# Gate products in three passes, modulations in batches of four, norms spread by transposes: a change to a two-layer diffusion backbone on one Trainium2 core

## The chip, the core and the metric

The kernel runs on one core of a Trainium2 chip. Its engines work in parallel, each through its own queue in order: TensorE (PE; its weight loads are listed apart as PEld), VectorE (DVE), ScalarE (ACT), GpSimd (POOL), and SyncE (SP), whose queue issues nearly all DMA transfers here. PE multiplies a stationary operand that is loaded first by a moving one and writes to banks of PSUM. The metric is device time in microseconds of one execution, the median of several runs; lower is better.

## The reference

The model has two layers over 512 latent tokens and 256 context tokens of width 1024. Each layer computes

```python
mod_x = (silu_c @ ada_w[l] + ada_b[l])[:, None, :]
sh1, sc1, gt1, sh2, sc2, gt2 = jnp.split(mod_x, 6, axis=-1)
mod_c = silu_cc @ ada_w[l] + ada_b[l]
...
ux = modulate(rmsnorm(x, norm1_g[l]), sh1, sc1) @ w_in[l]
uc = modulate(rmsnorm(ctx, norm1_g[l]), csh1, csc1) @ w_in[l]
...
mix_x = jnp.concatenate(
    [conformer_conv(ux[..., :CONV_IN], *cv), rwkv_out(yx, prep_x, *post)],
    axis=-1).astype(x.dtype)
...
x = x + gt1 * (mix_x @ w_out[l])
x = x + gt2 * swiglu(modulate(rmsnorm(x, norm2_g[l]), sh2, sc2),
                     ffn_wg[l], ffn_wu[l], ffn_wd[l])
```

`conformer_conv` is a depthwise convolution of 31 taps with a group norm; `rwkv_out` normalizes the output of a two-directional recurrence over the tokens by heads, adds a bonus, and multiplies by a gate `g = sigmoid(g_lo) @ g_up`, a product over 160 values (the head gate). The context has the same path in layer 0, and only feeds the recurrence's state in layer 1. A last RMS norm ends it. All values are float32.

Three pieces matter below: the modulations (`silu(c) @ ada_w`, for c and c_ctx at once: a product with two rows and 6144 columns in each layer), the head gate, and the norms, whose factor per token has to reach all 128 partitions.

## The kernel before

Activations lie with channels on partitions and tokens along the free dimension: 8 tiles of 128 channels by 768 tokens. Large products are made of three passes over rounded parts: an operand is split into a high part (`act` to a rounded type) and a low part (`tt`, the difference), and high x high, high x low and low x high are added up in PSUM (`dense`, `win`, `project`). Products given as plain float32 appear as two PE records for each call. `mm` (L234), `act` (L222), `stt` (L225), `tt` (L228) and `ts` (L231) are helpers, so those lines stand for nearly all instructions; tile names tell them apart.

The order of time, with the stages of the profile in us from its start:

- 0 to 75: inputs, norm, first modulations, first three input projections of layer 0.
- 75 to 645: layer 0's recurrent stage. Twelve batches (four pairs of heads by three token groups); a function `weave` interleaves lanes of PE work at positions written out in `PLAN`: the recurrence's steps (`chains`, 12 a batch), inversion of small triangular blocks, token transposes, input projections, convolutions, norms, modulations (`ada`, a number of steps for each batch). Inside `tc.manual_schedule` PE runs in exactly this order; the other engines' orders, and everything outside, come from a list scheduler that takes program order as priority. Toward the end `mix_early` multiplies by the head gates and `out_early` begins the output projection.
- 645 to 732: rest of the output projection, second norm, modulation, first feed-forward tile (outside the manual order).
- 732 to 1262: layer 0's feed-forward, in parts of 6, 6, 5 and 5 of its 22 tiles. For each tile f there are two products (gate and up, 24 x 2 PE products each), whose weight tiles (512 KB) are loaded by SP into two buffers and split by ACT and DVE into two more.
- 1262 to 2250: the same for layer 1 (recurrent stage 1310 to 1832, feed-forward from about 1876 on).

The parts that the change touches:

- Modulations (`ada_load` L280, `ada_sums`, `ada_cols`, `ada_steps`). The 48 column groups of 128 in each layer are computed one by one. SP loads a group's weights (128 partitions x 1024, 512 KB) in one DMA. `ada_sums` makes eight products with 32 stationary columns (c and c_ctx in two of them) over 128 moving columns; product k goes to partitions 32(k mod 4) onward of one bank, so that the eight partial sums stand in four places. ACT copies the bank to `ev`. `ada_cols` multiplies `ev` by `sel` (a 0/1 matrix with two columns), which adds the four places and turns columns into partitions, and DVE adds the bias (and for scales forms (1 + scale) x norm gain). A step of the generator is one of these two halves. Part 0 (16 groups: shift and scale before the mixer), part 1 (8, mixer's gate), part 2 (16, before the feed-forward), part 3 (8, feed-forward's gate). Layer 0's part 0 runs in the first stage; its parts 1 and 2 and layer 1's part 0 (40 groups) as a lane of layer 0's recurrent stage; layer 1's parts 1 and 2 (24) in its own; part 3 of each layer (`gates`, six buffers) is placed ahead of the feed-forward and run by `run(gates)`.
- Norms (`spread`, called by `rstd`, `gn`, `pair_prep`). A norm's sums are taken as products with tokens on partitions; an approximate inverse square root is computed there on small tiles and written out widely, and `spread` turns each 128 x 128 piece into channels on partitions by a float32 product with the identity matrix. Token tiles are turned by `PE.transpose` elsewhere in the kernel (L850, L862).
- Head gates (`mix_early`, `gate`). The gate's inputs were written to DRAM (`gd`) by the input projection. `gs` (2 tiles of 80 partitions) and `gu` (2 of 80 x 512) are loaded, and for each of four channel groups float32 products of depth 80 are summed into `w` banks; DVE multiplies the mixer's tiles by them, or ACT copies them for the last pair.

## Time and profile before

| what | us |
|---|---|
| median of 3 runs | 2247.91 |
| lowest, highest run | 2246.09, 2260.29 |
| the profiled execution | 2251.84 |
| its span, from first to last instruction | 2250.0 |

| engine | busy us in the profile | share | instructions |
|---|---|---|---|
| PEld | 1724.2 | 77% | 18800 |
| DVE | 1333.6 | 59% | 3249 |
| ACT | 952.3 | 42% | 2260 |

The mean clock granted to TensorE is 0.975 of the full one. In a row of a group view the columns are: line, engine, operation, output<-inputs by tile name, shapes, count | busy us, mean ns | idle time of the engine just before these instructions and what ended it. In the timeline they are: start, duration, engine, line, operation, tiles, shapes, count of merged instructions, and in brackets the idle time before and its releaser. A PE record's duration contains the pipeline's depth, so consecutive records overlap; the time that a product takes from PE is the distance between starts.

### The profile page before, as it was taken

Reading aid. Unit: us, or ns where it says so; the run is one execution under the profiler, and the core shown is the slowest. Engines: PE = TensorE matmul, PEld = TensorE weight load, DVE = VectorE, ACT = ScalarE, POOL = GpSimd, SP = SyncE. Lnnn points to the kernel's source line nnn. Section 1 sums busy time; section 2 is a strip of 40 time slices with the busy share of each in tenths; the row PEclk is TensorE's granted clock in tenths of the full one; section 3 lists DMA queues with packets and bytes.
Section 4 is the critical chain, followed back from the end, with each engine's and each line's share of the span. In section 5 each row is a group of like instructions: output and inputs, shape, how many; then the busy total and the mean of one; then the engine's idle time right before and its main releaser. Section 6 shows DMA issues by size and latency. Waiting matters only on the chain.

```text
span 2250.0 us, 46614 instructions
## 1 busy us (share of the span) xinstructions
PE 2134.0 (95%) x18800; PEld 1724.2 (77%) x18800; DVE 1333.6 (59%) x3249; ACT 952.3 (42%) x2260; POOL 193.0 (9%) x524
## 2 busy tenths in 40 slices
PE   6999999999999999999999999999999989999996
PEld 4777777777687888888888776767676678888885
DVE  5578887878648332332333766778777755343446
ACT  5455645555325211211212545566656534222223
POOL 0102121312010000000000000121212010000000
PEclk9999999999799999999999999899999999999999
DMA  8233422333554112111122413132424552223223
GB/s 289 65 100 90 108 77 68 84 98 107 146 176 150 57 52 71 61 61 66 51 72 86 139 49 94 37 84 66 114 52 116 169 204 75 95 90 106 86 98 118
DMA packets 196007, 220.72 MB, mean 98 GB/s; under 512 B 110352, under 2 KB 139792, under 8 KB 195792
## 3 DMA queue, kind: packets, MB, share of 16 engines
q1 hardware_dynamic: 194640, 215.65, 31.9%
q8 instruction: 148, 2.42, 0.4%
q10 hardware_dynamic: 1152, 2.10, 0.2%
q14 instruction: 67, 0.55, 0.1%
HBM read 192.49 MB, written 25.21 MB: 97 GB/s over the span
## 4 chain that ended last, share of the span: by engine, by line
PE 77%; ACT 8%; DVE 7%; DMA 3%; POOL 2%; issue 2%; SPq 0%; POOLq 0%; ACTq 0%; DVEq 0%
PE pd L234 38%; PE pw L234 33%; PE pc L234 5%; ACT tmp L222 2%; ACT UV L222 1%; DVE wl L228 1%; DMA raw<-in_wd 1%; DMA Dt<-d 1%; PE pw L862 1%; ACT wh L222 1%; DVE acc L225 1%; PE pw L850 1%; ACT Tm L222 0%; DVE xtmp L228 0%; POOL rq L385 0%
## 5 line engine op out<-in xcount | busy, mean ns | idle before, releaser
L234 PE MATMUL pd<-h,wh 128*128 128x512 f32 (+2 forms) x2496 | 686.5, 364 | 6.6 <-ACT h L222 4.5
L222 ACT ACTIVATE wh<-raw 128x1024 fp32r<-128x1024 f32 (+2 forms) x234 | 220.6, 944 | 714.1 <-PE pw L234 317.2
L234 PEld LDWEIGHTS pd<-h,wh 128*128 128x128 f32 (+1 forms) x2496 | 424.9, 190 | 80.0 <-ACT h L222 5.8
L234 PE MATMUL pd<-h,wl 128*128 128x512 f32 (+2 forms) x1248 | 426.6, 365 | 0.0
L228 DVE TENSOR_TENSOR wl<-raw,wh 128x1024 fp32r<-128x1024 f32 (+2 forms) x234 | 252.6, 1081 | 239.1 <-ACT wh L222 237.6
L234 PE MATMUL pw<-h,wh 128*128 128x512 f32 (+1 forms) x1264 | 316.4, 349 | 1.7 <-DVE x L225 1.7
L234 PEld LDWEIGHTS pd<-h,wl 128*128 128x128 f32 (+1 forms) x1248 | 223.8, 189 | 35.7 <-issue 1.6
L234 PEld LDWEIGHTS pw<-h,wh 128*128 128x128 f32 x1264 | 210.3, 189 | 37.3 <-DVE x L225 1.9
L225 DVE SCALAR_TENSOR_TENSOR acc<-z,cw,acc 128x497 f32<-128x497 f32 (+9 forms) x336 | 209.7, 644 | 2.1 <-ACT acc L222 1.4
L234 PE MATMUL pw<-h,wl 128*128 128x512 f32 (+1 forms) x632 | 193.4, 351 | 0.0
L234 PE MATMUL pd<-mid,wh 128*128 128x512 f32 (+1 forms) x568 | 136.6, 344 | 5.0 <-ACT wh L222 4.9
L228 DVE TENSOR_TENSOR ft<-ft,pw 128x512 f32<-128x512 f32 (+1 forms) x67 | 37.8, 590 | 171.2 <-PE pw L234 170.8
L234 PE MATMUL pw<-mid,wh 128*128 128x512 f32 (+1 forms) x568 | 136.5, 343 | 0.6 <-ACT wh L222 0.6
L234 PEld LDWEIGHTS pw<-h,wl 128*128 128x128 f32 x632 | 106.9, 189 | 15.3
L234 PEld LDWEIGHTS pd<-mid,wh 128*128 128x128 f32 x568 | 93.4, 189 | 20.6 <-ACT wh L222 6.5
L234 PEld LDWEIGHTS pw<-mid,wh 128*128 128x128 f32 x568 | 93.7, 189 | 14.4 <-ACT wh L222 0.8
L970 POOL TENSOR_TENSOR Q<-S,pc 128x128 f32<-128x128 f32 x80 | 44.7, 559 | 537.7 <-DVE S L225 183.5
L234 PE MATMUL pd<-mid,wl 128*128 128x512 f32 (+1 forms) x284 | 87.6, 347 | 2.3 <-DVE wl L228 2.3
L234 PE MATMUL pw<-mid,wl 128*128 128x512 f32 (+1 forms) x284 | 87.4, 346 | 0.6 <-DVE wl L228 0.6
L225 DVE SCALAR_TENSOR_TENSOR x<-pw,mod,x 128x512 f32<-128x512 f32 (+1 forms) x60 | 40.1, 672 | 80.4 <-PE pw L234 80.4
L228 DVE TENSOR_TENSOR xtmp<-XT,Dt 64x15 f32<-64x15 f32 (+4 forms) x360 | 75.3, 209 | 11.5 <-DMA Dt<-d 7.2
L774 POOL MEMSET tmp<- 128x4 f32 x48 | 5.2, 108 | 876.3 <-PE pw L234 632.3
(190 smaller groups left out, 3298.0 us busy)
## 6 DMA issues: line engine op xcount, KB each, us to landing
ada<-in_ada SPq DMA_DIRECT2D x96, 512.0 KB, 4.2
raw<-in_wgu SPq DMA_DIRECT2D x88, 512.0 KB, 3.4
raw<-in_win SPq DMA_DIRECT2D x42, 512.0 KB, 3.4
raw<-in_wd SPq DMA_DIRECT2D x48, 320.0 KB, 2.9
Tm<-dimg SPq DMA_DIRECT2D x96, 128.0 KB, 3.6
raw<-in_wd SPq DMA_DIRECT2D x32, 384.0 KB, 3.0
d<-G SPq DMA_DIRECT2D x96, 64.0 KB, 2.1
raw<-in_wo SPq DMA_DIRECT2D x16, 384.0 KB, 3.2
```

The costliest lines, as they stand in the source:

```text
L222: A.activation(out=out, in_=in_, func=func, **k)
L225: V.scalar_tensor_tensor(out=out, in0=in0, scalar=scalar, in1=in1, op0=op0, op1=op1, **k)
L228: V.tensor_tensor(out=out, in0=a, in1=b, op=op)
L234: PE.matmul(out=out, lhsT=lhsT, rhs=rhs, start=start, stop=stop)
L774: G.memset(lx[:, :, 0:1], 0.0)
L850: PE.transpose(pt[hh][:, o:o + 64], bk[hs, d, cc, hh:hh + 2, :].rearrange("p j t -> p (j t)"), ident[hs, hs])
L862: PE.transpose(pv[0:64, o:o + 128], src, ident)
L970: G.tensor_tensor(out=Q, in0=S, in1=pc[:, :, s:s + 1].to_broadcast([128, 2, 64]), op=MUL)
```

## The change

Modulations: four column groups go together (a "four"). The weights are laid out anew on the host, so that one 512 KB load holds a quarter of the depth (two of eight rows of blocks) for four groups; `ada_sums` writes group j to partitions 32j onward, eight products a load as before. With `kept` a bank is kept over the four loads and copied once; without it each load has a bank of its own, the first copied by ACT and the others added by DVE. `sel` has eight columns and one product serves four groups; biases and scales are done for two or four groups at a time. A generator step is one load's products. The first stage has eight buffers instead of six and needs a whole four (and the first quarter of the next) before the first modulation. Layer 0's recurrent stage computes its parts 1 and 2 only (6 fours). Layer 0's part 3 and all of layer 1's modulations (14 fours, 56 quarter steps) run in layer 0's feed-forward, two steps after each of the two products of a tile f > 0, with two load buffers and `c` banks of PSUM. Layer 1 computes none, and the part 3 ahead of both feed-forwards is gone.

Norms: `spread` uses `PE.transpose`. Head gates: `gu` and `gs` are split into high and low parts and multiplied in three passes; `gu` is one load through `load_split`, with its buffers.

```diff
+FOURS = [f for c in (0, 24) for f in [[c + i, c + i + 1, c + i + 8, c + i + 9] for i in (0, 2, 4, 6)]
+         + [list(range(c + 16 + i, c + 20 + i)) for i in (0, 4)]]
...
-    sel = np.zeros((128, 2), np.float32)
+    sel = np.zeros((128, 8), np.float32)
     for j in range(4):
-        sel[32 * j, 0] = sel[32 * j + 1, 1] = 1.0
+        sel[32 * j, 2 * j] = sel[32 * j + 1, 2 * j + 1] = 1.0
...
-         ada=(4, 4, 4, 3, 1, 3, 3, 3, 4, 3, 4, 4), dense=(1, 1, 0.75, 1, 1, 1, 1.6, 1),
+         ada=(2, 2, 2, 2, 2, 2, 2, 2, 2, 3, 2, 2), dense=(1, 1, 0.75, 1, 1, 1, 1.6, 1),
...
-         ada=(2, 1, 1, 1, 1, 5, 1, 2, 2, 3, 3, 2), dense=(1, 1, 1, 1, 1.25, 1, 0.8, 1),
+         ada=(0,) * 12, dense=(1, 1, 1, 1, 1.25, 1, 0.8, 1),
...
-    def ada_sums(raw, pool):
-
-        ps = bank("d")
-        for k in range(8):
-            q = k % 4
-            mm(ps[32 * q:32 * q + 32, 0:128], cs[:, k, :], raw[:, 128 * k:128 * k + 128], k < 4, k >= 4)
-        ev = pool.tile([128, 128], F32, tag="ev", name=nm("ev"), bufs=2)
-        act(ev, ps[:, 0:128])
-        return ev
+    def ada_sums(ps, q, raw, start, stop):
+
+        for k in range(2):
+            for j in range(4):
+                mm(ps[32 * j:32 * j + 32, 0:128], cs[:, 2 * q + k, :], raw[:, 512 * k + 128 * j:512 * k + 128 * j + 128],
+                   start and k == 0, stop and k == 1)
...
-        mm(pt[:, 0:2], ev, sel)
...
+        mm(pt[:, 0:8], ev, sel)
...
-                mm(pt[:, c - c0:c - c0 + 128], wide[:, c:c + 128], ident)
+                PE.transpose(pt[:, c - c0:c - c0 + 128], wide[:, c:c + 128], ident)
...
+        for i in range(len(todo)):
+            for q in range(4):
+                if q == 0 or not kept:
+                    ps = bank(tag)
+                ada_sums(ps, q, raws[4 * i + q], q == 0 or not kept, q == 3 or not kept)
+                load()
+                if q == 0 and i:
+                    end(i - 1)
+                if q == 3 if kept else q == 0:
+                    ev = pool.tile([128, 128], F32, tag="ev", name=nm("ev"), bufs=2)
+                    act(ev, ps[:, 0:128])
+                elif not kept:
+                    tt(ev, ev, ps[:, 0:128], ADD)
+                yield
+        end(len(todo) - 1)
+        yield
...
-            ada0 = first.enter_context(tc.tile_pool(name="ada0", bufs=6))
-            ada = ada_steps([(0, 0)], ada0, 6)
+            ada0 = first.enter_context(tc.tile_pool(name="ada0", bufs=8))
+            ada = ada_steps([(0, 0)], ada0, 8, kept=True)
...
-                    for i in range(min(32, max(12, 4 * k + 6)) - done):
+                    for i in range(min(17, 4 * (k // 2) + 5 + 2 * (k % 2)) - done):
...
-            gs, gu = [], []
+            gu = load_split(I["gup"][l], rows=80)
+            gs = []
             for j in range(2):
-                t = hp.tile([128, T], F32, tag="h", name=nm("gs"))
-                nc.sync.dma_start(out=t[:80, :NE], in_=gd[j, :, :NE])
-                gs.append(t)
-                t = hp.tile([128, T], F32, tag="h", name=nm("gu"))
-                nc.sync.dma_start(out=t[:80, 0:RW], in_=I["gup"][l, :, RW * j:RW * j + RW])
-                gu.append(t)
+                hl = hpair()
+                nc.sync.dma_start(out=hl[1][:80, :NE], in_=gd[j, :, :NE])
+                act(hl[0].bitcast(F32R)[:80, :NE], hl[1][:80, :NE])
+                tt(hl[1].bitcast(F32R)[:80, :NE], hl[1][:80, :NE], hl[0][:80, :NE], SUB)
+                gs.append(hl)
...
-                for pt, a, b in ps:
-                    for j in range(2):
-                        mm(pt[:, 0:b - a], gu[j][:80, 128 * p:128 * p + 128], gs[j][:80, a:b], j == 0, j == 1)
+                for j in range(2):
+                    for n in range(3):
+                        for pt, a, b in ps:
+                            mm(pt[:, 0:b - a], gu[n // 2][:80, RW * j + 128 * p:RW * j + 128 * p + 128],
+                               gs[j][n % 2].bitcast(F32R)[:80, a:b], j == 0 and n == 0, j == 1 and n == 2)
...
-        ada = ada_steps([(l, 1), (l, 2)] + ([] if last else [(1, 0)]), s1, 1)
+        ada = iter(()) if last else ada_steps([(l, 1), (l, 2)], s1, 1)
...
-        gctx = ExitStack()
-        gates = ada_steps([(l, 3)], gctx.enter_context(tc.tile_pool(name=f"gates_{l}", bufs=6)), 6)
...
-        run(gates)
-        gctx.close()
...
+        adaf = iter(()) if last else ada_steps([(l, 3)] + [(l + 1, j) for j in range(4)],
+                                               fctx.enter_context(tc.tile_pool(name=f"adaf_{l}", bufs=2)), 2, "c", True)
...
+                        for _ in range(2):
+                            next(adaf, None)
...
+        run(adaf)
```

More of the change, by code (lines that the diff above doesn't have):

```diff
@@ L41 @@
 NPRM = _o
-NCST = 128 * 3 + 2 + 256
+NCST = 128 * 3 + 8 + 256
 O1 = 1024 + 3 * RW
@@ L109, in _pack @@
     x["cvec"] = np.stack([_cols(a["c"][0]), _cols(a["c_ctx"]), _cols(a["final_g"])], 2).reshape(128, 24)
-    x["ada"] = a["ada_w"].reshape(DEPTH, 8, 128, 48, 128).transpose(0, 3, 2, 1, 4).reshape(DEPTH, 48, 128, 1024)
+    aw = a["ada_w"].reshape(DEPTH, 4, 2, 128, 48, 128)[:, :, :, :, [g for f in FOURS for g in f]]
+    x["ada"] = aw.reshape(DEPTH, 4, 2, 128, 12, 4, 128).transpose(0, 4, 1, 3, 2, 5, 6).reshape(DEPTH, 12, 4, 128, 1024)
     w = a["w_in"].reshape(DEPTH, 8, 128, -1)
@@ L248, in net @@
     cst = cp.tile([128, NCST], F32, name="cst")
-    nc.sync.dma_start(out=cst[:, 0:386], in_=I["cst"][:, 0:386])
+    nc.sync.dma_start(out=cst[:, 0:392], in_=I["cst"][:, 0:392])
     prm = cp.tile([128, DEPTH * NPRM], F32, name="prm")
@@ L252, in net @@
     ident, blk, cen = (cst[:, 128 * j:128 * j + 128] for j in range(3))
-    sel = cst[:, 384:386]
-    gmask = cst[:, 386:642].rearrange("p (h u j) -> p h u j", h=2, u=1)
+    sel = cst[:, 384:392]
+    gmask = cst[:, 392:648].rearrange("p (h u j) -> p h u j", h=2, u=1)
     eps = cp.tile([128, 4], F32, name="eps")
@@ L276, in net, with ada_load @@
     ts(cs[:, :, 0:2], cth, 0.5, 0.0)
[L278 removed]
+    def ada_load(l, n, q, pool, bufs):
         raw = pool.tile([128, 1024], F32, tag="a", name=nm("ada"), bufs=bufs)
[L280 removed]
+        nc.sync.dma_start(out=raw, in_=I["ada"][l, n, q])
         return raw
[L283 to L291 removed]
@@ new lines, in ada_cols @@
+    def ada_cols(l, n, mod, sc, c0, ev):
+        g, two = FOURS[n][0] - c0, sc is not None
+        pt = bank("w")
+        mm(pt[:, 0:8], ev, sel)
+        o = l * NPRM + PRM["ada_b"][0] + c0
+        bias = prm[:, o:o + (16 if two else 8)]
+        if not two:
+            tt(mod[:, g:g + 4, :], pt[:, 0:8].rearrange("p (k c) -> p k c", c=2),
+               bias[:, g:g + 4].unsqueeze(2).to_broadcast([128, 4, 2]), ADD)
+            return
+        for j in range(2):
+            tt(mod[:, 8 * j + g:8 * j + g + 2, :], pt[:, 4 * j:4 * j + 4].rearrange("p (k c) -> p k c", c=2),
+               bias[:, 8 * j + g:8 * j + g + 2].unsqueeze(2).to_broadcast([128, 2, 2]), ADD)
+        o = l * NPRM + PRM["n1" if c0 == 0 else "n2"][0] + g
+        stt(sc[:, g:g + 2, :], mod[:, 8 + g:10 + g, :], 1.0,
+            prm[:, o:o + 2].unsqueeze(2).to_broadcast([128, 2, 2]), ADD, MUL)
@@ L305, in load_split @@
+    def load_split(ap, n=1024, pool=None, rows=128):
         raw = wp.tile([128, 1024], F32, tag="w", name=nm("raw"))
-        nc.sync.dma_start(out=raw[:, :n], in_=ap)
+        nc.sync.dma_start(out=raw[:rows, :n], in_=ap)
         hi = (pool or wh_p).tile([128, 1024], F32R, tag="wh", name=nm("wh"))
-        act(hi[:, :n], raw[:, :n])
+        act(hi[:rows, :n], raw[:rows, :n])
         lo = (pool or wh_p).tile([128, 1024], F32R, tag="wl", name=nm("wl"))
-        tt(lo[:, :n], raw[:, :n], hi[:, :n].bitcast(F32), SUB)
+        tt(lo[:rows, :n], raw[:rows, :n], hi[:rows, :n].bitcast(F32), SUB)
@@ L469, in ada_start @@
         mods[l, part] = mod, sc, c0
-        return [c0 + 8 * j + i for i in range(8) for j in range(n // 8)]
+        return [i for i, f in enumerate(FOURS) if c0 <= f[0] < c0 + n]
     def ada_end(l, part):
@@ L512, in late_constants @@
     def late_constants():
-        nc.sync.dma_start(out=cst[:, 386:NCST], in_=I["cst"][:, 386:NCST])
+        nc.sync.dma_start(out=cst[:, 392:NCST], in_=I["cst"][:, 392:NCST])
         lm = tmp_("lm")
@@ L1192, in lane @@
                     lanes.append((*plan["lanes"][name], n, gen))
-                lanes = [(0, 16, nproj, proj, filler), (0, 16, 2 * plan["ada"][b], ada)]
+                lanes = [(0, 16, nproj, proj, filler), (0, 16, plan["ada"][b], ada)]
                 lane("chains", chains(b), 12)
```

38 lines of the change are left out of this document (11 added, 27 removed).

## The prediction

> **What bounds the kernel.** I read the page's engine shares first, then busy time by stage (a table of windows: their length, then busy us of PE, weight loads, DVE, ACT and POOL, the clock granted to TensorE, DMA share, GB/s), then the timeline of the places that the change touches.
>
> ```profile
> PE 2134.0 (95%) x18800; PEld 1724.2 (77%) x18800; DVE 1333.6 (59%) x3249; ACT 952.3 (42%) x2260; POOL 193.0 (9%) x524
> 75.00:645.00 570.00, 536.81 (x6644) 419.45 (x6644) 443.43 (x1272) 303.80 (x860) 102.51 (x243) 0.95 0.35 96
> 645.00:732.00 87.00, 83.44 (x588) 70.64 (x588) 62.45 (x139) 39.44 (x74) 4.27 (x14) 0.98 0.47 166
> 732.00:1262.00 530.00, 530.00 (x2978) 458.66 (x2977) 181.20 (x250) 113.06 (x151) 0.00 (x0) 1.00 0.22 70
> 1310.00:1832.00 522.00, 496.66 (x5851) 368.27 (x5850) 369.34 (x1065) 300.62 (x848) 84.98 (x257) 0.97 0.34 92
> 1832.00:1876.00 44.00, 37.98 (x360) 32.61 (x359) 34.90 (x104) 26.35 (x64) 0.00 (x0) 1.00 0.48 170
> ```
>
> PE is the bound everywhere. The two recurrent stages (75 to 645 us in layer 0, 1310 to 1832 in layer 1) leave it idle 33 and 25 us, while DVE has 78% and 71%. The first feed-forward (732 to 1262) leaves it idle for nothing. So work taken off PE is worth its own length less the waits that come out from under it, and work put into the feed-forward costs its full length. The change does both, and the sum is the difference.
>
> **A modulation group's price.** Rows of the timeline (start, duration, engine, line, operation; one PE record's length is latency, so I price by start to start):
>
> ```profile
> 690.54 0.40 PE L234 MATMUL pw<-h,wh 128*128 128x256 f32 x2
> 690.78 0.28 PE L234 MATMUL pw<-h,wl 128*128 128x256 f32 x1
> 690.99 0.64 PE L234 MATMUL pd<-ada,cs 128*32 128x128 f32 x16
> 691.56 0.50 PE L234 MATMUL pw<-h,wh 128*128 128x256 f32 x2
> 691.90 0.28 PE L234 MATMUL pw<-h,wl 128*128 128x256 f32 x1
> ...
> 26.77 1.28 PE L234 MATMUL pd<-ada,cs 128*32 128x128 f32 x32
> 28.02 0.38 PE L234 MATMUL pw<-cst,ev 128*128 128x2 f32 x2
> 28.34 0.54 PE L234 MATMUL pd<-ada,cs 128*32 128x128 f32 x12
> ...
> 40.42 0.28 PE L234 MATMUL pw<-cst,ev 128*128 128x2 f32 x2
> 40.56 0.59 PE L234 MATMUL pd<-h,wh 128*128 128x512 f32 x2
> ...
> ada<-in_ada SPq DMA_DIRECT2D x96, 512.0 KB, 4.2
> ```
>
> Eight products (16 records) take 0.57 us. The product before them holds 0.21 instead of 0.12, the two after them 0.34 instead of 0.24: 0.76 us for one group among dense work. Two groups together take 1.25, so a pair costs 1.44. The selecting product (ev by sel) costs 0.32 among modulations and 0.14 in dense work; I take 0.28 in the recurrent stages. There are 96 groups before and 96 quarter-steps after: the streaming is the same, and only 72 of the 96 selections go.
>
> - Layer 0's recurrent stage: 40 groups become 24 steps: 16 x 0.76 = 12.2; 40 selections become 6: 34 x 0.28 = 9.5. Together 21.7. ACT loses 34 evictions, DVE gets 18 additions for some 50 small column operations: nothing on the path.
> - Layer 1's recurrent stage: 24 x 0.76 + 24 x 0.28 = 24.9 go, with their loads on SP's queue.
> - First feed-forward: 14 fours, 56 steps in 28 pairs: 28 x 1.44 + 14 x 0.32 = +45. PE has no gap there, so all of it counts; the bounds are 40, a few steps falling into the waits before it, and rival 5.
> - First stage: 12 of 16 selections go; the first four needs five loads instead of two. I take -2, from +2 to -4.
>
> The feed-forward's new loads pass through SP ahead of weight loads:
>
> ```profile
> 740.53 0.33 SPq L306 DMA_DIRECT2D raw<-in_wgu  x1
> 746.67 1.06 ACT L222 ACTIVATE wh<-raw 128x1024 fp32r<-128x1024 f32 x1 [6.66 <-PE pw L234]
> 755.31 0.86 PE L234 MATMUL pw<-h,wh 128*128 128x512 f32 x4
> ```
>
> A weight tile is issued at 740.5, split from 746.7 and used at 755.3: 14.8 us ahead. A modulation load waits in that queue until PE has read its buffer, which PE does between two dense blocks; it would have to hold SP for some 6 us to be felt. I cost it at nothing. Cover gone, each of 28 pairs would cost what SP holds over that.
>
> **Spreads.** These are 26 by rstd, 80 by group norms, 48 by kk, in 128-column pieces:
>
> ```profile
> L862 PE MATMUL pw<-cst,vr 128*64 128x128 f32 x96 | 23.6, 273 | 0.0
> L234 PE MATMUL pw<-cst,gsq 128*128 128x128 f32 x160 | 23.3, 296 | 8.3 <-POOL gsq L386 7.6 <-ACT rv L222 0.7
> 671.56 1.50 PE L234 MATMUL pw<-cst,gsq 128*128 128x128 f32 x12
> 672.82 0.70 PE L234 MATMUL pd<-h,wh 128*128 128x512 f32 x2
> ...
> 548.26 1.60 PE L234 MATMUL pw<-cst,gsq 128*128 128x128 f32 x12 [0.85 <-POOL gsq L386]
> 549.80 0.68 PE L234 MATMUL pw<-Tm,G 64*64 64x64 f32 x16
> ...
> 556.15 0.27 PE L862 MATMUL pw<-cst,vr 128*64 128x128 f32 x1
> 556.25 0.27 PE L862 MATMUL pw<-cst,v 128*64 128x128 f32 x1
> ```
>
> 80 group-norm spreads leave 160 records: two each, (1.26 to 1.54)/6 = 0.21 to 0.26 us. The token transposes leave one record for each of their 96 calls, at 0.10 us. Their weights have 64 columns, the spread's 128, so the new price is not shown; its bounds are 0.10 and, nothing gained, 0.23 (weights and moving columns stay what they are, which excludes a loss). I take 0.11, nearer the transposes, which run the same operation: 0.12 saved each, 8.6 us in layer 0's recurrent stage (72), 6.7 in layer 1's (56), 2.4 elsewhere (20, outside the first stage). [...]
>
> **Head gates.**
>
> ```profile
> 570.82 3.75 PE L234 MATMUL pw<-gs,gu 80*128 80x512 f32 x6 [2.60 <-DMA gu<-in_gup]
> 576.14 5.49 PE L234 MATMUL pw<-gs,gu 80*128 80x512 f32 x8
> 581.55 0.69 PE L234 MATMUL pc<-KR,S 64*64 64x64 f32 x8
> 570.00:600.00 30.00, 29.18 (x133) 16.77 (x134) 15.84 (x29) 7.40 (x18) 0.63 (x1) 0.50 0.56 155
> ...
> 1757.88 1.98 PE L234 MATMUL pw<-gs,gu 80*128 80x512 f32 x4
> 1759.70 0.28 PE L234 MATMUL pw<-cst,ev 128*128 128x2 f32 x2
> ```
>
> Layer 0's four gates take 5.41 us each, because TensorE has half its clock from 570 to 600. Three passes over 768 columns in two halves are six times 0.36 (three 256-column products in the rows above): 2.2 us at full clock, 4.3 at half. All cold saves 4.3 in all; all warm 13, and up to 4 more on what lies between. What comes late next: the second gate tile lands after the same write, then ACT and DVE must split it (some 0.85 and 0.95 us) before PE goes on, with 1.1 us of the first half to cover them; ACT and DVE stand behind that load too. I take two gates cold and two warm and 10 us in all; bounds 3 to 15. Layer 1's cost 1.82 and will cost 1.44: 1.5 in all, its gate tiles come early.
>
> [...]
>
> **The feed-forward gates** that ran before each feed-forward, 8 groups and 8 selections, 8 x 0.76 + 8 x 0.28 = 8.3 us of PE at each of two places:
>
> ```profile
> 695.00 0.95 PE L234 MATMUL pc<-eps,acc 128*128 128x1 f32 x8
> 703.63 1.16 PE L234 MATMUL pc<-cst,rstd 128*128 128x128 f32 x8
> 708.56 0.50 PE L234 MATMUL pd<-h,wh 128*128 128x512 f32 x1 [1.48 <-ACT h L222]
> ...
> 2241.84 1.20 PE L234 MATMUL pc<-cst,rstd 128*128 128x128 f32 x4 [2.71 <-DVE rstd L225]
> ```
>
> They filled part of the wait for the norm: 8.6 us from sums to spread, where the last norm of the kernel has 2.7 us of wait alone. With them gone PE will wait there, some 3 us. I take 4.5 saved at each place, 9 in all (bounds 2, the wait merely bare, and 16.6, all of it).
>
> **Sum.** In the recurrent stages I let 75% pass in layer 0 (DVE at 78% is next) and 80% in layer 1: 0.75 x (21.7 + 8.6) = 22.7; 0.8 x (24.9 + 6.7 + 1.5) = 26.5. Then -2 - 22.7 - 26.5 - 10 - 9 - 2.4 + 45 = -27.6. The profiled execution took 2251.8 (span 2250.0), 3.9 above the median: 2224 for it, and 2220 against the median of 2247.9. I say 2221.
>
> **Rivals.** (1) Waits take the place. The work removed was filler between steps of the recurrence whose ACT and DVE operations are late already; if only 45% passes in both stages, 21 us come back: 2242. For it: 58 us of idle PE that is spread over many short waits, and DVE at 78%. Against it: PE is 94 and 95% busy there, so few places are without cover. (2) The change doesn't do what it says: a 128-column transpose takes as long as the two records. That returns 0.12 x 154, after the shares some 14 us: 2235. For it: the spread's weight load is twice the tokens'. Against: one record for two. [...] (5) Slower: the feed-forward's order is not written by hand, and modulations are cut into pieces:
>
> ```profile
> 1843.97 0.41 PE L234 MATMUL pd<-ada,cs 128*32 128x128 f32 x2
> 1844.31 0.51 PE L234 MATMUL pw<-h,wh 128*128 128x256 f32 x2
> ```
>
> Two records alone hold PE 0.34 us, and 0.19 more with the changeovers: 0.53 a piece. Four pieces a step make 56 x 4 x 0.53 = 119 instead of 40: +79, 2300. It decides (over 1% slower) from three pieces a step. For it: those rows; against: most groups before the first feed-forward ran whole, and the new ones stand ahead of the next dense block in program order.
>
> **How the numbers follow.** Forecast 0.41, (1) 0.30, (2) 0.11, (3) 0.04, (4) 0.06, (5) 0.08. A difference under about 1% (22 us) can hardly be told from none here. Faster by over 1% is below 2225.4: 0.51 (nearly all of the forecast, (3) and (4), and what of (1) passes more); slower by over 1% is (5) with three pieces or more: 0.07; within 1%: 0.42. The forecast's own range is 2205 to 2234; the one that holds 8 in 10 reaches from 2203 past (2) and (1) to 2247, and leaves out (5), some of (1) and the tail below.
>
> **What would show it.** In the changed profile: the first feed-forward longer by 40 to 50 us, its modulation records in runs of 16 and 32; the recurrent stages shorter by 25 to 40 and by 20 to 32; spreads with one record each at 0.10 to 0.13 us; gate products of layer 0 at about 2.2 us and the low clock shorter than 30 us; 24 selections. The prediction is wrong if a recurrent stage keeps its length, or if the feed-forward shows idle PE or pieces of two.

## The result and the profile after

The changed kernel takes 2261.7 us (median of 20 runs) against 2250.2 us for the kernel before (20 runs beside them): a ratio of 1.0055, with a 95% interval from 1.004 to 1.007. It is half a per cent slower. One of its 20 runs took 4458 us and does not enter the ratio. The forecast was 2221 us, with 2247 as the upper end.

The profiled execution took 2261.3 us and has a span of 2259.5 us; like the profiled execution of the kernel before (2251.8), it lies within 2 us of its kernel's median. Its page gives the engine shares, and a table of windows gives the same stages as before (length, then busy us of PE, weight loads, DVE, ACT and POOL, the granted clock, DMA share, GB/s). The windows are shifted with their stages: layer 0's recurrent stage, what stands between it and the feed-forward, the first feed-forward, layer 1's recurrent stage, and the way to the second feed-forward.

```profile
PE 2116.3 (94%) x18526; PEld 1701.7 (75%) x18526; DVE 1326.0 (59%) x3201; ACT 940.8 (42%) x2194; POOL 203.6 (9%) x524
```

```profile
74.00:626.00 552.00, 511.18 (x6281) 398.53 (x6282) 442.61 (x1252) 299.06 (x829) 105.56 (x243) 0.95 0.31 84
626.00:712.00 86.00, 79.48 (x458) 68.04 (x457) 61.79 (x131) 38.92 (x67) 4.26 (x14) 0.94 0.39 132
712.00:1274.00 562.00, 562.00 (x3864) 478.73 (x3862) 182.41 (x279) 114.48 (x164) 0.00 (x0) 1.00 0.34 116
1325.00:1850.00 525.00, 485.76 (x5381) 354.81 (x5380) 369.14 (x1038) 299.15 (x828) 91.58 (x253) 0.94 0.26 69
1850.00:1888.00 38.00, 29.57 (x201) 27.70 (x202) 31.27 (x94) 22.82 (x53) 0.00 (x0) 0.87 0.23 77
```

Layer 0's recurrent stage became 18 us shorter and the first feed-forward some 32 us longer, as was meant. The surprise is layer 1's stage (fourth row): it issues 470 matmul records fewer than before and is 3 us *longer*, because PE's idle time rose from 25 to 39 us and its mean clock fell from 0.97 to 0.94.

For finer marks I use the first and last product `pc<-Z,Tm` of each layer's chain of recurrence steps ("chain" below; it lies inside the recurrent stage), and the last product on `mid` tiles of the first feed-forward:

| section (us) | before | after | difference |
|---|---|---|---|
| start to the first chain step of layer 0 | 149.5 | 147.5 | -2.0 |
| chain of layer 0 | 494.6 | 477.7 | -16.9 |
| from there to the end of the first feed-forward | 640.3 | 673.3 | +33.0 |
| to the first chain step of layer 1 | 96.8 | 97.5 | +0.7 |
| chain of layer 1 | 428.3 | 431.3 | +3.0 |
| from there to the end | 440.5 | 432.2 | -8.3 |

The differences add up to the 9.5 us between the spans.

**Where layer 1's gain went.** Up to chain step 86 of 96 (48 belong to layer 1) the changed kernel gains 15 us on the kernel before; between steps 86 and 92 it gives 17 back. Windows of the same 27 us, before and after:

```profile
1752.00:1779.00 27.00, 26.40 (x348) 17.66 (x342) 24.96 (x70) 14.32 (x42) 1.84 (x3) 1.00 0.48 149
```

```profile
1752.00:1779.00 27.00, 25.81 (x197) 18.65 (x199) 15.76 (x50) 11.89 (x35) 2.64 (x2) 0.50 0.18 55
```

PE is equally busy in both, but at half clock after the change, and so gets through 197 records instead of 348. The timeline of PE there (start, duration, records; in brackets the idle time before and what ended it):

```profile
1753.00 0.69 PE L870 MATMUL pw<-cst,bk 64*128 64x64 f32 x7 [1.09 <-ACT Tm L226]
...
1760.34 1.22 PE L238 MATMUL pw<-h,wh 80*128 80x512 f32 x2
1761.36 0.63 PE L238 MATMUL pw<-h,wl 80*128 80x512 f32 x1
1761.79 1.05 PE L238 MATMUL pw<-h,wh 80*128 80x512 f32 x2
1762.64 0.63 PE L238 MATMUL pw<-h,wl 80*128 80x512 f32 x1
1763.20 0.70 PE L238 MATMUL pc<-UV,G 128*64 128x64 f32 x8
...
1775.13 1.22 PE L238 MATMUL pd<-h,wh 128*128 128x512 f32 x2
...
1790.57 0.47 PE L238 MATMUL pw<-Tm,G 64*64 64x64 f32 x2 [5.10 <-DMA Tm<-dimg]
```

A three-pass gate takes 2.86 us here (1760.34 to 1763.20), more than the 1.82 that the four-pass gate took at full clock before. The clock comes back only at 1779.5, 4.4 us after the row at 1775.13, the first products of 512 columns over 128 rows. The wait of 5.10 us is the other part of the loss. All engines' rows show what it waits for:

```profile
1782.53 0.17 DVE L232 TENSOR_TENSOR XT<-XT,xtmp 64x15 f32<-64x15 f32 x1
...
1782.76 2.15 SPq L913 DMA_DIRECT2D dimg<-XT  x2
...
1783.66 0.64 ACT L226 ACTIVATE XT<-XT 64x256 f32<-64x256 f32 x1
...
1786.92 2.58 SPq L921 DMA_DIRECT2D Tm<-dimg  x4
```

The last inverse of a block (`XT`) is a row of small steps on DVE, in order with the multiplications that wait for PE's gates. With PE slow it ends at 1782.5 (1768.5 before the change), and its image is back from memory only at 1790. In the run pad, below, with the clock at 0.97 from 1749 to 1776, the wait ends at 1776.09 and not at 1790.57, and it is 5.07 us long.

### The profile page after: what moved, and what is told of

It reads as the page before. It is cut to its first block, busy times and chain, and to the rows that moved or that the text cites. A ratio compares the mean times of both kernels' runs of the same rounds, so it can differ in the third digit from the quotient of the medians.

```text
span 2259.5 us, 45907 instructions
## 1 busy us (share of the span) xinstructions
PE 2116.3 (94%) x18526; PEld 1701.7 (75%) x18526; DVE 1326.0 (59%) x3201; ACT 940.8 (42%) x2194; POOL 203.6 (9%) x524
## 4 chain that ended last, share of the span: by engine, by line
PE 74%; ACT 9%; DVE 9%; POOL 3%; issue 2%; DMA 2%; SPq 0%; POOLq 0%; ACTq 0%; DVEq 0%
PE pd L238 35%; PE pw L238 30%; PE pc L238 6%; ACT tmp L226 2%; ACT UV L226 1%; DVE acc L229 1%; DVE wl L232 1%; DMA raw<-in_wd 1%; PE pw L882 1%; PE pw L403 1%; ACT wh L226 1%; ACT W L226 1%; POOL rq L395 1%; PE pw L870 1%; ACT G L226 1%
## 5 line engine op out<-in xcount | busy, mean ns | idle before, releaser
L238 PE MATMUL pw<-h,wh 128*128 128x512 f32 (+3 forms) x1312 | 341.8, 360 | 4.6 <-DVE x L229 1.9
L238 PEld LDWEIGHTS pw<-h,wh 128*128 128x128 f32 (+1 forms) x1312 | 224.1, 195 | 43.6 <-DVE x L229 3.1
L238 PE MATMUL pw<-h,wl 128*128 128x512 f32 (+2 forms) x656 | 203.5, 356 | 0.0
L238 PEld LDWEIGHTS pw<-h,wl 128*128 128x128 f32 (+1 forms) x656 | 114.9, 195 | 17.8
L990 POOL TENSOR_TENSOR Q<-S,pc 128x128 f32<-128x128 f32 x80 | 50.9, 637 | 535.6 <-DVE S L229 233.8
```

The source lines that it names most:

```text
L238: PE.matmul(out=out, lhsT=lhsT, rhs=rhs, start=start, stop=stop)
L990: G.tensor_tensor(out=Q, in0=S, in1=pc[:, :, s:s + 1].to_broadcast([128, 2, 64]), op=MUL)
```

## The experiments

Two tables are used throughout. The first gives the medians, each against the kernel before on the same chip:

| kernel | us | ratio to before (95%) |
|---|---|---|
| no_g: changed, four-pass gates | 2259.7 | 1.0041 (1.0018 to 1.0064) |
| g_only: before + three-pass gates | 2246.8 | 0.9990 (0.9973 to 1.0007) |
| t_only: before + transposed spreads | 2244.8 | 0.9984 (0.9970 to 0.9997) |
| m_back: changed, parts 1 and 2 of layer 1 back | 2235.6 | 0.9953 (0.9936 to 0.9970) |
| m_back3: the same with part 3 of layer 1 | 2235.2 | 0.9932 (0.9907 to 0.9956) |
| dup: changed, those parts computed twice | 2263.0 | 1.0045 (1.0025 to 1.0065) |
| m_end: as m_back, steps in the last batches | 2262.9 | 1.0049 (1.0029 to 1.0069) |
| pad: changed, gates over 128 rows | 2252.9 | 1.0015 (0.9994 to 1.0036) |
| before_pad: before, gates over 128 rows | 2232.3 | 0.9933 (0.9910 to 0.9956) |
| back_pad: m_back and pad | 2237.2 | 0.9950 (0.9930 to 0.9970) |
| pre_pad: back_pad, parts 3 ahead of the feed-forwards | 2227.4 | 0.9902 (0.9882 to 0.9922) |
| stay_pad: pre_pad, no part in the feed-forward | 2231.4 | 0.9915 (0.9892 to 0.9939) |

The second splits the two chains of each profiled execution: PE's idle time (gaps between its rows), what half clock cost (half of the time that PE was busy while the clock stood at 0.5), and the rest, which is PE's work at full clock. The half is an estimate from the changed kernel's timeline: single products of 512 columns begin 0.43 us apart at 0.50 (686.60 to 690.01) and 0.23 at 1.00 (690.75 to 696.21).

| chain, kernel | length | idle | half clock | work |
|---|---|---|---|---|
| layer 0: before | 494.6 | 29.6 | 25.5 | 439.5 |
| changed | 477.7 | 37.3 | 22.3 | 418.2 |
| t_only | 495.7 | 32.7 | 31.6 | 431.4 |
| dup | 485.5 | 38.1 | 30.5 | 416.9 |
| before_pad | 484.3 | 30.9 | 12.7 | 440.6 |
| pre_pad | 475.3 | 40.5 | 15.2 | 419.7 |
| stay_pad | 482.4 | 36.9 | 19.5 | 426.0 |
| layer 1: before | 428.4 | 21.9 | 13.6 | 392.9 |
| before, second profile | 440.2 | 21.6 | 27.1 | 391.5 |
| changed | 431.3 | 35.2 | 26.1 | 370.0 |
| no_g | 433.4 | 30.3 | 32.9 | 370.2 |
| t_only | 426.1 | 23.3 | 15.1 | 387.6 |
| m_back | 427.6 | 28.7 | 11.6 | 387.2 |
| dup | 424.5 | 28.8 | 8.0 | 387.7 |
| m_end | 445.1 | 38.4 | 21.7 | 385.0 |
| pad | 417.3 | 35.0 | 9.1 | 373.3 |

One caution for the second table. The changed kernel and dup have the same instructions in the same order on all engines through layer 0, and yet that chain took 477.7 us in one profile and 485.5 in the other, with 22.3 and 30.5 us lost to half clock. So single profiles differ by some 8 us through the clock alone; the medians decide, and the profiles show by what.

### First: which part of the change loses the time

Theory G said that the new gates lose it, rival F that the missing modulations do: they had been cover, that is work that filled PE's waits.

**no_g**, the changed kernel with four-pass gates over unsplit tiles:

```diff
-                for j in range(2):
-                    for n in range(3):
-                        for pt, a, b in ps:
-                            mm(pt[:, 0:b - a], gu[n // 2][:80, RW * j + 128 * p:RW * j + 128 * p + 128],
-                               gs[j][n % 2].bitcast(F32R)[:80, a:b], j == 0 and n == 0, j == 1 and n == 2)
+                for pt, a, b in ps:
+                    for j in range(2):
+                        mm(pt[:, 0:b - a], gu[j][:80, 128 * p:128 * p + 128], gs[j][:80, a:b], j == 0, j == 1)
```

> The changed kernel with the head gates back in four passes over unsplit tiles; modulations and spreads stay changed. Theory G (the three-pass gates themselves lose the time at the end of layer 1's recurrent stage: their parts are split on DVE and ACT ahead of the block inverses, and the products run at half clock): the 17 us lost from chain step 86 to 92 of layer 1 come back, layer 0's gates cost about 4 us more; 2249 us. Rival F (the modulations that left layer 1's last batches were the cover; the gates only stand where the gap opens): the loss stays, and four passes at half clock add about 3 us in layer 1 and 4 in layer 0; 2268 us.

The profile shows the loss as before, with a half-clock stretch of 27.3 us from 1750. The median, 2259.7 us, lies between G's number and F's. The runs spread more widely than those of the other kernels: six of 12 took 2262.7 to 2266.6 us, the profiled one (2263.0) among them, and six 2236.5 to 2256.7 at a higher mean clock (0.968 to 0.978 against 0.960 to 0.964). So the profile speaks against G, and the next run decides.

**g_only**, the reverse of that diff in the kernel before.

> The kernel before with the three-pass head gates alone. Theory G: layer 1's recurrent stage grows by 12 to 17 us between chain steps 86 and 92, layer 0 gains about 4; 2260 us. Rival F: the modulations still fill layer 1's last batches, so its gates stay at full clock and the part gains about 4 us in layer 0 and 1 in layer 1; 2245 us.

2246.8 us: F's side, and G, which asked for 2260, falls. Three passes are worth 2 us, with an interval from 6 us to none.

**t_only**, one line in the kernel before:

```diff
-                mm(pt[:, c - c0:c - c0 + 128], wide[:, c:c + 128], ident)
+                PE.transpose(pt[:, c - c0:c - c0 + 128], wide[:, c:c + 128], ident)
```

> The kernel before with the spreads by transposes alone. If the predicted shares pass (0.75 and 0.8 of 8.6 and 6.7 us, and 2.4 elsewhere): 14 us less, 2236 us. If about half passes, as the whole change showed in the recurrent stages: 10 us less, 2240. If the released time is all given back to waits: 2250.

4 us, not 10 or 14. The operation does what was predicted; this is a row of six spreads in t_only's timeline, which took 1.26 to 1.54 us before:

```profile
552.21 0.82 PE L393 MATMUL pw<-cst,gsq 128*128 128x128 f32 x6
```

The table of chains says where the time went: PE's work falls by 8.1 us in layer 0 and 5.3 in layer 1, and layer 0's chain is as long as before, with 3.1 us more idle time and 6.1 more at half clock. Most of that half clock stands at one place, behind layer 0's fourth spread of a group norm. Windows of t_only, then of the kernel before, the spread beginning in the first of each pair (same columns as above):

```profile
416.20:419.60 3.40, 2.42 (x31) 2.12 (x31) 2.93 (x9) 0.53 (x2) 0.99 (x2) 1.00 0.18 39
419.60:423.00 3.40, 3.40 (x32) 2.75 (x32) 1.32 (x3) 0.73 (x3) 1.66 (x8) 0.50 0.14 20
...
416.40:419.80 3.40, 2.17 (x19) 1.57 (x15) 2.78 (x8) 0.62 (x2) 2.84 (x6) 1.00 0.17 35
419.80:423.20 3.40, 3.40 (x53) 3.00 (x54) 3.04 (x6) 0.56 (x2) 0.29 (x1) 1.00 0.05 10
```

In t_only the clock stays at half for 10.2 us there. All eleven profiles with transposed spreads have such a stretch, of 3.4 to 17.1 us, that begins 0.5 to 5.8 us after this spread does; none of the four with spreads as products has one, although PE is no busier in the first window there than in t_only's (2.17 us against 2.42). Whether the transposes themselves bring the clock down, no run shows.

**m_back**, the 24 steps of layer 1's parts 1 and 2 back in layer 1's stage:

```diff
-         ada=(0,) * 12, dense=(1, 1, 1, 1, 1.25, 1, 0.8, 1),
+         ada=(2, 2, 2, 2, 2, 2, 2, 2, 2, 3, 2, 2), dense=(1, 1, 1, 1, 1.25, 1, 0.8, 1),
...
-        ada = iter(()) if last else ada_steps([(l, 1), (l, 2)], s1, 1)
+        ada = ada_steps([(l, 1), (l, 2)], s1, 1)
...
-        adaf = iter(()) if last else ada_steps([(l, 3)] + [(l + 1, j) for j in range(4)],
+        adaf = iter(()) if last else ada_steps([(l, 3), (l + 1, 0), (l + 1, 3)],
```

> The changed kernel with parts 1 and 2 of layer 1's modulations (six fours, 24 steps) back in layer 1's recurrent stage, two steps a batch as in layer 0; the first feed-forward keeps the other eight fours. The feed-forward loses 24 steps at the 0.61 us measured in it: 14.6 us less. Layer 1's recurrent stage pays 20 us of PE work, of which some half passes: 10. Theory G: the loss of 17 us at the gates stays; 2257 us. Rival F: the cover is back, the 17 us return too; 2240 us.

2235.6 us, 26 less than the changed kernel. Most of it is not layer 1's: in the profiles 21.0 us come from the section of the first feed-forward (652.4 against 673.4 us), where 14.6 were expected for the 24 steps that left it. Most of the rest is in the pace of its large products (see the last section). But G asked layer 1's chain to grow by some 10 us and F asked it to shrink by some 7; it does 17 us more work on PE and is 4 us shorter, which is F's side. The rows of the chain, changed kernel and m_back:

```profile
1396.00:1828.00 432.00, 396.37 (x4774) 283.60 (x4773) 311.72 (x902) 257.53 (x738) 83.46 (x222) 0.94 0.25 63
```

```profile
1371.00:1799.00 428.00, 399.25 (x5170) 285.68 (x5168) 315.71 (x929) 259.12 (x743) 81.60 (x222) 0.97 0.35 92
```

### Second: is it cover, and what holds the clock

**dup**: the change of m_back in layer 1, with its steps in the plan, but the feed-forward keeps all fours, so the work is done twice.

```diff
+        keep = dict(mods)
-        ada = iter(()) if last else ada_steps([(l, 1), (l, 2)], s1, 1)
+        ada = ada_steps([(l, 1), (l, 2)], s1, 1)
...
             run(ada)
+            if last:
+                mods.update(keep)
```

> The changed kernel, which computes parts 1 and 2 of layer 1's modulations a second time in layer 1's recurrent stage (two steps a batch, the copy is not used); the feed-forward keeps all 14 fours. It is the changed kernel plus 20 us of PE work and 24 loads. Theory F (cover): the added work lies in PE's waits and keeps the clock up at the gates; no slower than the changed kernel's 2261.7 us, about 2250. Rival H (all that the kernel with the parts moved back won was the shorter feed-forward): the stage pays the usual half to 0.8 of 20 us; 2272 to 2278 us.

2263.0 us: the 17.7 us of added PE work cost about 1 us, so rival H falls, but the 11 us that F promised did not come. In the profile layer 1's chain is 6.8 us shorter than the changed kernel's and layer 0's 7.8 longer, in unchanged instructions. Shown is that the steps cost next to nothing in layer 1, not that they win.

**m_end**: as m_back, all 24 steps in the last batches.

```diff
-         ada=(2, 2, 2, 2, 2, 2, 2, 2, 2, 3, 2, 2), dense=(1, 1, 1, 1, 1.25, 1, 0.8, 1),
+         ada=(0, 0, 0, 0, 0, 0, 0, 0, 1, 8, 8, 8), dense=(1, 1, 1, 1, 1.25, 1, 0.8, 1),
```

> The changed kernel with parts 1 and 2 of layer 1's modulations back in layer 1's recurrent stage as before, but all 24 steps in its last batches (8 to 11), beside the gates, and none in batches 0 to 7. Theory F with the clock as the cause: batches 0 to 9 keep the 15 us that they gained in the changed kernel, the end does not lose 17; about 2228 us, less than the 2235.6 with the same steps spread over all batches. Rival K (the stage is bound by its recurrence, not by PE: its length is the same wherever the steps lie): 2235 us or more.

2262.9 us, 35 above F's number. Nothing like the long half-clock stretch stands at the gates (the clock is 0.98 from 1736 to 1816), but layer 1's chain loses 25 us on the kernel before from step 84 on. Against the changed kernel it has 15.0 us more work and is 13.8 longer: two steps a batch fit in (dup), eight cost nearly their full price. K's number holds, but its premise falls, since the chain's length (445.1 us against 427.6 in m_back) does depend on where the steps lie. Another 9.4 us of the distance to m_back stand in layer 0's chain, whose code is the same, with 13.5 us more at half clock there; why is open.

**m_back3**: part 3 of layer 1 in layer 1's stage as well (against m_back).

```diff
-         ada=(2, 2, 2, 2, 2, 2, 2, 2, 2, 3, 2, 2), dense=(1, 1, 1, 1, 1.25, 1, 0.8, 1),
+         ada=(2, 2, 3, 3, 3, 3, 3, 3, 3, 3, 3, 2), dense=(1, 1, 1, 1, 1.25, 1, 0.8, 1),
...
-        ada = ada_steps([(l, 1), (l, 2)], s1, 1)
+        ada = ada_steps([(l, 1), (l, 2)] + ([(l, 3)] if last else []), s1, 1)
...
-        adaf = iter(()) if last else ada_steps([(l, 3), (l + 1, 0), (l + 1, 3)],
+        adaf = iter(()) if last else ada_steps([(l, 3), (l + 1, 0)],
```

> Parts 1, 2 and 3 of layer 1's modulations (eight fours, 32 steps) in layer 1's recurrent stage, two to three steps a batch; the feed-forward keeps six fours. Theory F: eight steps more are hidden in the waits of that stage, and the feed-forward loses 8 x 0.61 us; 2230 us against 2235.6. Rival H: the stage pays what the feed-forward saves; 2235 us.

2235.2 against 2235.6: H's number, but the profiles don't show H's reason. The feed-forward's section is 6.2 us shorter than in m_back and layer 1's chain only 1.5 longer; the rest is lost in layer 0's chain, in unchanged code, with 4.5 us more at half clock. The ratios' intervals overlap as well, so whether a third step a batch is still free stays open.

**pad**: the gates' operands are cleared in rows 64 to 127 first and multiplied over all rows; the numbers of products and columns stay.

```diff
+        if zero:
+            G.memset(hi[64:128, :n].bitcast(F32), 0.0)
...
+        if zero:
+            G.memset(lo[64:128, :n].bitcast(F32), 0.0)
...
-            gu = load_split(I["gup"][l], rows=80)
+            gu = load_split(I["gup"][l], rows=80, zero=True)
...
+                for t in hl:
+                    G.memset(t[64:128, :NE], 0.0)
...
-                            mm(pt[:, 0:b - a], gu[n // 2][:80, RW * j + 128 * p:RW * j + 128 * p + 128],
-                               gs[j][n % 2].bitcast(F32R)[:80, a:b], j == 0 and n == 0, j == 1 and n == 2)
+                            mm(pt[:, 0:b - a], gu[n // 2][:, RW * j + 128 * p:RW * j + 128 * p + 128],
+                               gs[j][n % 2].bitcast(F32R)[:, a:b], j == 0 and n == 0, j == 1 and n == 2)
```

> The changed kernel with the gate products over all 128 rows, of which rows 80 to 127 are zeros in both operands: as many products of as many columns. Theory R (the clock stays at half through the gates because these products use 80 of 128 rows): the half-clock stretch at layer 1's gates shrinks from 27.3 us to under 10 and layer 0's from 30.7 too; 2248 to 2252 us. Rival S (what counts is something else, such as zeros not counting, or the small products between the gates): both stretches stay; 2260 us, and perhaps 2 more for the zeroing.

2252.9 us, 9 less than the changed kernel: theory R. Layer 1's 27.3 us at half clock are gone, layer 0's 30.7 are 13.7 and 3.4. Windows of layer 1's gates and the 27 us behind them, and of layer 0's gates, in pad:

```profile
1749.00:1776.00 27.00, 21.15 (x251) 15.65 (x251) 24.20 (x66) 12.61 (x38) 2.22 (x3) 0.97 0.37 101
1776.00:1803.00 27.00, 26.34 (x334) 19.11 (x334) 11.44 (x28) 11.34 (x32) 1.97 (x3) 0.90 0.28 86
...
556.00:587.00 31.00, 26.89 (x276) 20.24 (x272) 27.51 (x68) 13.82 (x36) 3.60 (x3) 0.72 0.58 169
```

The first row is less busy than the same stretch of the changed kernel (21 of 27 us against 26) and still at 0.97. So a busier PE did not go with a higher clock here. The wait for the last inverse is still there:

```profile
1776.09 0.47 PE L238 MATMUL pw<-Tm,G 64*64 64x64 f32 x2 [5.07 <-DMA Tm<-dimg]
```

It goes with the missing modulations and not with the clock (5.10 us behind 27.3 us at half clock in the changed kernel, 5.07 here with the clock at 0.97): the longest wait there is 3.71 us in no_g, 1.2 to 2.7 in the six kernels with two or three steps a batch back in layer 1's stage, and in the kernels that have layer 1's modulations as before, and in m_end, there is none.

### Third: the rows alone, and what is best

**before_pad**: the same padding in the kernel before, whose gates have four passes.

```diff
+                G.memset(t[64:128, :NE], 0.0)
...
+                G.memset(t[64:128, 0:RW], 0.0)
...
-                        mm(pt[:, 0:b - a], gu[j][:80, 128 * p:128 * p + 128], gs[j][:80, a:b], j == 0, j == 1)
+                        mm(pt[:, 0:b - a], gu[j][:, 128 * p:128 * p + 128], gs[j][:, a:b], j == 0, j == 1)
```

> The kernel before with its four-pass gate products over all 128 rows, rows 80 to 127 zeros. Theory R (products that use 80 of 128 rows leave the clock at half): layer 0's half-clock stretch at the gates shrinks from 30.7 us to 17 or less, half of what goes is time: 7 us; layer 1's gates had full clock already; 2242 us. Rival S: the stretch stays at 30 us; 2249.

2232.3 us, 16 less than before. Layer 0's half-clock stretch is 6.8 us (the window from 568 to 585 stands at 0.80), and of its gates (PE's timeline) the first still stands at half clock, while the next three take 2.85 to 3.05 us where each took 5.49:

```profile
569.19 3.75 PE L234 MATMUL pw<-gs,gu 128*128 128x512 f32 x6 [2.94 <-DMA gs<-gd]
574.51 3.05 PE L234 MATMUL pw<-gs,gu 128*128 128x512 f32 x8
578.10 2.85 PE L234 MATMUL pw<-gs,gu 128*128 128x512 f32 x8
581.61 2.85 PE L234 MATMUL pw<-gs,gu 128*128 128x512 f32 x8
```

Layer 0's chain is 10.3 us shorter, and 12.8 us less at half clock account for all of it. Another 7.8 us come from the first feed-forward, whose code is the same; see the last section. The two profiles are 23 us apart where the medians are 16, so how the 16 divide isn't known exactly: some 10 us at the gates are shown to be the padding's, and for the rest it is not shown.

**back_pad**, the edits of m_back and pad together:

> The changed kernel with both edits: parts 1 and 2 of layer 1's modulations back in layer 1's recurrent stage, and the gate products over 128 rows. If the clock at the gates and the length of the feed-forward are two separate causes, and the stretch in layer 0 (30.7 us) shrinks as it did with the padding alone: 5 us less than the 2235.6 of the first edit; 2230. If the padding only mends what the missing cover opened: 2235 to 2237.

2237.2 against 2235.6: they don't add up. In layer 1's chain either one alone has less half clock in these profiles (11.6 us in m_back and 9.1 in pad, 26.1 in the changed kernel); layer 0's stretch at the gates fell to 13.7 and 3.4 us, but layer 0's chain lost 28.4 us to half clock in all in this execution, some 20 of them away from the gates.

**pre_pad**: back_pad with the parts 3 ahead of their feed-forwards (against back_pad).

```diff
+        gates = ada_steps([(l, 3)], gctx.enter_context(tc.tile_pool(name=f"gates_{l}", bufs=6)), 6, kept=True)
...
+        run(gates)
+        gctx.close()
-        adaf = iter(()) if last else ada_steps([(l, 3), (l + 1, 0), (l + 1, 3)],
+        adaf = iter(()) if last else ada_steps([(l + 1, 0)],
```

> As the kernel with both edits, and besides the feed-forward gates (parts 3, two fours for each layer) ahead of their own feed-forwards again; layer 0's feed-forward keeps only part 0 of layer 1 (four fours). Theory W (those groups were cover for the wait between norm and feed-forward, where the clock now drops for 10.2 us in either layer): the feed-forward loses 16 steps, 10 us, and the two places pay 1 us each; 8 us less than the kernel with both edits: 2222. Rival (they pay 4.5 us each, as the prediction took): 2229.

2227.4 us, 10 less than back_pad, where W asked for 8 less and the rival for 1: theory W by the difference, though the number itself is nearer the rival's, since back_pad stood at 2237 and not at 2230. From layer 0's last chain step to its last `mid` product it is 12.4 us shorter, and from layer 1's last chain step to its first `mid` product, where work came back, 2.1 shorter. The wait ahead of layer 1's spread, 3.46 us in back_pad, is gone. This is the fastest kernel of the study, 1% under the kernel before.

**stay_pad**: pre_pad with part 0 of layer 1 in layer 0's stage again (against pre_pad).

```diff
-         ada=(2, 2, 2, 2, 2, 2, 2, 2, 2, 3, 2, 2), dense=(1, 1, 0.75, 1, 1, 1, 1.6, 1),
+         ada=(4, 4, 4, 3, 1, 3, 3, 3, 4, 3, 4, 4), dense=(1, 1, 0.75, 1, 1, 1, 1.6, 1),
...
-        ada = ada_steps([(l, 1), (l, 2)], s1, 1)
+        ada = ada_steps([(l, 1), (l, 2)] + ([] if last else [(1, 0)]), s1, 1)
...
-        adaf = iter(()) if last else ada_steps([(l + 1, 0)],
+        adaf = iter(())
```

> Every part of the change but the move: modulations in batches of four where the kernel before had them (part 0 of layer 1 in layer 0's recurrent stage, parts 1 and 2 in their own, parts 3 ahead of their feed-forwards), spreads by transposes, three-pass gates over 128 rows. Against the kernel that has only part 0 of layer 1 in the feed-forward (2227.4 us): the feed-forward loses 16 steps, 10 us. Theory B (layer 0's recurrent stage pays 0.8 of 16 x 0.76 us): the same within 2 us, 2226 to 2229; the move as such is worth nothing. Rival (the steps lie in waits, as in layer 1): 2218.

2231.4 us: theory B within the intervals, which overlap. Its terms are borne out only in part: layer 0's chain is 7 us longer (9.7 were asked), but the feed-forward's section only 1 us shorter instead of 10, mostly because its large products ran at the slower of the two paces in the last section. So what the move alone is worth in layer 0 could not be told from nothing.

**before_again**, the kernel before profiled a second time:

> The kernel before, profiled a second time, to see which differences between single profiles belong to the execution and not to a kernel. If the feed-forward's dense products (177 ns from one record to the next in the kernel before, 173 in the kernel with padded four-pass gates, in the same code) differ by execution, a second look may show 173; if they belong to the build, 177 again, and layer 0's first feed-forward 469 to 471 us long. The half-clock stretch of 30 us at layer 0's gates should stand there again.

Between the first chain step of layer 0 and that of layer 1 every section agrees with the first profile within 0.3 us. The start is 3.3 us shorter, so the 2.0 us that the change seemed to win there can't be told from none. Layer 1's chain takes 440.2 instead of 428.4 us: a half-clock stretch of 30.7 us stands at the gates, which the first profile did not have. One gate in PE's timeline of the first profile, and the four of the second:

```profile
1757.88 1.98 PE L234 MATMUL pw<-gs,gu 80*128 80x512 f32 x4
```

```profile
1756.20 3.78 PE L234 MATMUL pw<-gs,gu 80*128 80x512 f32 x4
1760.76 3.78 PE L234 MATMUL pw<-gs,gu 80*128 80x512 f32 x4
1765.52 3.78 PE L234 MATMUL pw<-gs,gu 80*128 80x512 f32 x4
1771.30 3.78 PE L234 MATMUL pw<-gs,gu 80*128 80x512 f32 x4
```

So the long stretch in layer 1 is a trap that an execution falls into or not. The runs fit this: of 29 of the kernel before (those beside no_g), 25 took 2242.9 to 2251.5 us with mean clocks of 0.975 to 0.980, and four 2258.9 to 2261.2 with 0.970 to 0.973; the second profile, 2258.8 us and 0.971, is like the four. With gates of 80 rows and modulation steps beside them, one profile of eight shows it; with those steps taken out, two of two (the changed kernel and no_g); with 128 rows none of five, the steps in or out. These are few, and that the missing steps make the trap more likely is a reading, not a proof. What tips the clock ahead of the gates wasn't tried; the last wait before it was 1.09 us in the changed kernel and 1.02 in the kernel before, which kept its clock.

## Why the prediction was wrong

**The step that failed** is "0.8 x (24.9 + 6.7 + 1.5) = 26.5" for layer 1. The work did leave PE, if less of it: 22.9 us in the chain, where 33.1 were counted for the stage. But idle time grew by 13.3 us and half clock cost 12.5 more, so that none of it passed. Rival 1 named the first half of this (waits take the place of removed filler): by the idle time alone 9.6 of the 22.9 us would have passed, 42%, where it said 45%. Nothing in the prediction had the second half: it treated the clock as a matter of layer 0's gates, and took from the windows that layer 1 stood at 0.97 without asking what kept it there. In pad, with the gates over 128 rows, layer 1's chain is 11.1 us shorter than before: 19.6 less work, 13.1 more idle time, 4.5 less at half clock. The clock term belongs to executions as well as to kernels: against the second profile of the kernel before, which fell into the trap too, the changed chain is 9 us shorter.

**Layer 0's stage** was to gain 22.7 and 10 and gained 16.9. PE's work fell by 21.3 us, not by 30.3 and the gates' part: the selections had lain in waits in part (7.4 us of PE's idle time in the chain stood directly ahead of them, and none ahead of the five that are left), and only 54 of the 72 spreads lie in the chain. Of the 21.3, 7.7 came back as idle time, so that a share of 0.64 passed where 0.75 was taken; 3.2 us less at half clock make up the 16.9.

**Layer 0's gates** were taken as two at half clock and two at full, an estimate of the author's that neither the kernel before nor the changed one shows. All four ran at half clock: rows of one gate, 565.04 to the next one's 570.23, of the changed kernel:

```profile
565.04 1.65 PE L238 MATMUL pw<-h,wh 80*128 80x512 f32 x4
566.49 0.84 PE L238 MATMUL pw<-h,wl 80*128 80x512 f32 x2
567.12 1.48 PE L238 MATMUL pw<-h,wh 80*128 80x512 f32 x4
568.40 0.84 PE L238 MATMUL pw<-h,wl 80*128 80x512 f32 x2
...
570.23 1.65 PE L238 MATMUL pw<-h,wh 80*128 80x512 f32 x4
```

The price of a gate at half clock was right: 4.3 us predicted, 4.2 measured (565.04 to the end of the row at 568.40). In before_pad, over 128 rows, only the first gate stood at half clock (six of its records took 3.75 us, the eight of each later one 3.05, 2.85 and 2.85). Over 80 rows the clock was not back before the fourth gate ended: that gate ended at 594.8 in the kernel before, with four passes, and the clock was back at 600.7; in the changed kernel, with three, it was 580.6 and 584.8.

**The spreads** cost what was predicted, one record each and 0.10 to 0.13 us; 154 x 0.12 us were right for PE (13.4 us less work in the two chains of t_only) and wrong for the kernel, which gained 4 us of an expected 14. What the sum had at nothing was the clock behind them: 10.2 us at half clock at one place of t_only. Rival 2 (no gain from the operation) falls by the row of t_only: the row of six that took 1.50 to 1.60 us takes 0.82 here, and start to start 0.57 to 0.81 us against 1.26 to 1.54: a factor of about two.

**The feed-forward** was to cost 45 us and cost 34.7 (start to start, 30.4 for the steps and 4.3 for the selections); the section is 33.0 longer. The steps ran whole, so rival 5 falls:

```profile
723.71 1.08 PE L238 MATMUL pc<-ada,cs 128*32 128x128 f32 x32
724.73 0.97 PE L238 MATMUL pd<-h,wh 128*128 128x512 f32 x4
```

A pair takes 1.02 us here, not 1.44; 14 pairs ran together so, and 26 steps singly at 0.57 us. The changeover that was charged to each pair, from rows of half-width products, hardly exists between full ones.

**The feed-forward gates** were to save 4.5 us at each place. Some 7 us are seen behind layer 1's chain with its spreads. But pre_pad puts the groups back and pays little for them (there it is 2.1 us shorter than back_pad and 2.7 longer than the changed kernel): they were cover for the wait between norm and feed-forward (3.81 us ahead of layer 0's spread and 3.46 ahead of layer 1's in the changed kernel, and 10.2 us at half clock in either layer). Moved into a stage without idle time they cost 0.6 us a step.

Taken together: +9.5 measured in the profile, -27.6 predicted. Layer 1's chain is 29.5 us of the difference and layer 0's 15.8; the feed-forward and the rest, which came out better than predicted, give 8 back.

## What to carry to other kernels

Idle time of the bound engine is a place to put work for next to nothing (17.7 us of it cost 1 us in dup): before moving work out of a stage, see whether it lies in waits there, and before moving it into another, whether that one has any. A removal can have a second price in the clock: 12.5 us in layer 1 here, beside 13.3 of idle time. Where the clock had fallen at gates over 80 rows, it stood at 0.50 for 27 to 31 us. Padding those products to the full depth with zeros took 8 memsets here and, alone, made the kernel before 0.7% faster (some 10 of the 16 us at the gates), where the three edits together made it 0.5% slower.

## What was not expected of the hardware

- Rows of zeros shortened a half-clock stretch. At the gates over 80 rows the clock stood at 0.50 for 27 to 31 us in layer 0 in all ten profiles that have them, with PE busy for 29 of 30 us in the kernel before; over 128 rows, 48 of them zero, the stretch was 6.8 us (before_pad) to 17 us with a break (pad). The number of products and columns was the same. Gates over 80 rows were not always slow: in layer 1 of the first profile of the kernel before the same four ran at 1.00 throughout (1752 to 1779).
- With transposes in place of products the clock came down behind one spread in eleven of eleven profiles, and with products in none of four, though PE was about as busy there (2.42 us in t_only's window of 3.40 us and 2.17 in that of the kernel before; see t_only above).
- The first feed-forward's large products ran at two paces in the same code, all at clock 1.00. From one start to the next, products of 512 columns on `h` tiles took 236 ns (median) in both profiles of the kernel before, in g_only and in stay_pad, and 230 or 231 in t_only, before_pad and pre_pad. That is 470 to 471 against 462 to 463 us for the stretch between first and last `mid` product. In the changed kernel it was 236 while modulations ran and 232 after them. Two profiles of one kernel agree, so it seems to go with the build rather than the execution; why is open.
